# A hybrid RWKV-7 and attention encoder layer: TensorE's order written out for the scan and the attention, both scan directions in one stage, value products one key tile behind their transposes

## The chip, the cores and the metric

The kernel runs on one core of one Trainium2 chip. The metric is device time in microseconds (us). A NeuronCore has five engines that each run their own list of instructions: TensorE (PE in the profile; PEld is its loading of stationary operands), VectorE (DVE), ScalarE (ACT), GpSimd (POOL) and SyncE (SP, which here only issues transfers). They meet through semaphores.

## The reference

One encoder layer over 2304 tokens (a prompt of 256 and a sample of 2048, independent of each other), width 1024. After an RMSNorm and an input projection, half of the columns go through a bidirectional RWKV-7 scan (8 heads of 64), the other half through grouped-query attention (8 query heads, 2 key heads). Then output projection, SwiGLU FFN and norms. The parts that the change touches:

```python
def step(S, inp):                                   # forward and reverse, 8 heads
    r_t, w_t, k_t, v_t, a_t, b_t = inp
    sa = jnp.einsum('bhvk,bhk->bhv', S, a_t)
    S = S * w_t[:, :, None, :] + sa[..., None] * b_t[:, :, None, :] + v_t[..., None] * k_t[:, :, None, :]
    return S, jnp.einsum('bhvk,bhk->bhv', S, r_t)
...
y = y_f + y_b
...
s = jnp.einsum('bqhgd,bkhd->bhgqk', q_blk, k).astype(jnp.float32) * scale
p = jax.nn.softmax(s, axis=-1).astype(v.dtype)
return jnp.einsum('bhgqk,bkhd->bqhgd', p, v)
```

## The kernel before

`build` (L1276) runs in stages: input projection with the preparation of the scan (`e_phase`), the scan with attention beside it, what is left of attention, and the FFN. Stages are Python generators. `beside(g, rate)` (L1328) advances attention by `rate` steps for each step of `g`, so the two are woven together in the source. The source order is not the final one: the tile layer is opened with a scheduler that orders every engine's list by its own model of durations (L1396).

**The scan.** The tokens are 36 chunks of 64 (32 of the sample, then 4 of the prompt). Step k treats one chunk forward and another one backward. For each direction `scan_prep` (L624) loads the chunk's operands, makes the Gram products (L657, eight matmuls into two PSUM tiles `g`), masks them on VectorE (L661, L663) and transposes `bk` (L668). `scan_chain` (L686) is the serial part: for each direction four stages of eight 64-wide matmuls into that direction's half of `hb`: L705, then a ScalarE copy, L711, two copies, L717, the new state on VectorE (L720, L722), and the output L730 with L733. `scan_sv` (L672) sets the state as the next step's operand. `scan_out` (L752) normalizes finished tiles.

**The block inverses.** A chunk needs the inverse of a triangular matrix. `inverses` (L610) makes them for ten (block group, direction) pairs, one after the other: 62 dependent small operations on VectorE or GpSimd (L565, L567), a copy (L570), a round trip through DRAM, and four groups of products (L597, a mask L599, L604). The next pair takes over the previous one's buffers, so that it starts after the last L597. Pairs (0, 0) and (4, 1) are needed at the first chunk, (1, 0) and (3, 1) at the seventh, (3, 0) and (1, 1) at the nineteenth. `scan` pulls the generator `back` three times per round, and empties it as far as needed where a chunk's inverse is missing (L810).

**Attention.** For a key head and a tile of 128 queries, `att_scores` (L853) walks over 16 units (4 key blocks x 4 heads; a prompt tile has 4). A unit is two score products (L880, L881) into `as`, a maximum (L882, VectorE) and an exponential (L884, ScalarE). Then come small softmax operations (L890 to L897), and GpSimd scales the 16 results `p` (L901). `att_values` (L904) takes 128 keys at a time: four transposes into `at` (L913), a split into a high part (ScalarE, L175) and a low part (VectorE, L181), two products into `ao` (L916 with the high, L917 with the low part). `as` and `at` have two PSUM buffers each. `attention` (L927) takes one value step of the previous tile after each score unit.

Of the kernel before, what the change touches and what calls it, by code (L numbers as in the profile page):

```python
# [43 lines left out]
RATE_E, RATE_S = 1.0, 2.75  # L44
# [52 lines left out]
class Kern:  # L97
# [308 lines left out]
    def e_dir(self, e, p, d):  # L406
# [52 lines left out]
        for c in range(nch):  # L459
            for h in range(2):  # L460
# [5 lines left out]
        pool.tensor_scalar(out=self.wc[d][:, p, ch0:ch0 + nch], in0=e1[:, :nch, 64 - 64 * d], scalar1=1.0, scalar2=0.0,  # L466
                           op0=ALU.mult, op1=ALU.add)
# [156 lines left out]
    def scan_prep(self, d, c, sb, ps):  # L624

        nc = self.nc
        act, dve = nc.scalar, nc.vector
        bi, j = self.blk(c)
        gr, off = BLOCKS[bi][2:]
        cs = slice(j * P, j * P + P)  # L630
        q_ = self.sq = getattr(self, "sq", {})
# [3 lines left out]
        ar = self.ard[d][bi]  # L635
        cl = T("cl", [P, 2, 4, P], 4)
        for e in range(2):
            rows = slice(e * 64, e * 64 + 64)
            self.ld(cl[rows, e], ar[:, rows, cs].rearrange("q p t -> p q t"))
        bk = T("bk_", [P, 4, P], 2)  # L640
        self.ld(bk, self.bkd[d][bi][:, :, cs].rearrange("q p t -> p q t"))
        x = T("x_", [P, 4, C], 3)
        for e in range(2):
            self.ld(x[e * 64:e * 64 + 64], self.xd[d][gr][:, e, off + j].rearrange("q s t -> s q t"))
        sav = T("sav", [P, 4, 2, C], 3)
        v = self.vtd[bi][j * C:(j + 1) * C, :]
        self.ld(sav[64:128].rearrange("p q e c -> p (q e c)"), v)
        gm = self.c["gmask_" + "fb"[d]]
        mrb = T("mrb", [C, 4, 2, C], 4)
        bkt = T("bkt", [P, 4, P], 3)  # L650
        q_[d, c] = dict(cl=cl, x=x, sav=sav, mrb=mrb, bkt=bkt, v=v.rearrange("t (q e c) -> t q e c", e=2, c=C))
        yield
# [5 lines left out]
        for e in range(2):  # L658
            other = slice(64 - e * 64, 128 - e * 64)
            psg = psgs[e]  # L660
            dve.tensor_tensor(out=cl[other, e], in0=psg[64:128], op=ALU.mult,  # L661
                              in1=gm[64:128].rearrange("p (o t) -> p o t", o=1).broadcast_to([64, 4, P]))
            dve.tensor_tensor(out=mrb[:, :, e, :], in0=psg[0:64, :, 64:128], op=ALU.mult,  # L663
                              in1=gm[0:64, 64:128].rearrange("p (o t) -> p o t", o=1).broadcast_to([64, 4, C]))
            yield
        psg = ps.tile([P, 4, P], F32, name="g", tag="g", bufs=2)
        for q in range(4):
            nc.tensor.transpose(psg[:, q, :], bk[:, q, :], self.ident)  # L668
        act.copy(out=bkt, in_=psg)
        yield  # L670

    def scan_sv(self, d, c, st, sb):  # L672

        sv = sb.tile([P, 4, 2, C], F32, name="sv", tag=f"sv{d}", bufs=2)
        v = self.sq[d, c]["v"]
        self.ld(sv[64:128, :, 0, :], v[:, :, 0, :])
        self.ld(sv[0:64, :, 1, :], v[:, :, 1, :])
        if st[0] is None:
            st[0] = sb.tile([P, 4, C], F32, name="sc", tag=f"sc{d}", bufs=2)
            self.nc.gpsimd.memset(st[0], 0.0)  # L680
        self.nc.scalar.copy(out=sv[0:64, :, 0, :], in_=st[0][0:64])
        self.nc.gpsimd.tensor_scalar(out=sv[64:128, :, 1, :], in0=st[0][64:128], scalar1=1.0, scalar2=0.0, op0=ALU.mult,
                                     op1=ALU.add)
        st[1] = sv

    def scan_chain(self, d, c, nxt, st, first, sb, ps):  # L686
# [3 lines left out]
        o = self.sq[d, c]  # L690
        cl, x, sav, mrb, bkt = (o[k] for k in ("cl", "x", "sav", "mrb", "bkt"))

        def T(tag, shape, bufs):
            return sb.tile(shape, F32, name=tag, tag=tag, bufs=bufs)
        if st[1] is None:
            self.scan_sv(d, c, st, sb)
        sv = st[1]
        heads = [(h // 2, h % 2, slice(h % 2 * 64, h % 2 * 64 + 64)) for h in range(8)]

        
        def H():
            return self.hb[:, d]
        psa = H()
        for q, e, rows in heads:
            nc.tensor.matmul(psa[rows, q, :], cl[:, e, q, 0:64], sv[:, q, e, :], start=True, stop=True)  # L705
        ry = T("ry", [P, 4, C], 2)
        act.copy(out=ry, in_=psa)
        yield
        psx = H()
        for q, e, rows in heads:  # L710
            nc.tensor.matmul(psx[rows, q, :], x[rows, q, :], ry[rows, q, :], start=True, stop=True)  # L711
        act.copy(out=sav[0:64, :, 0, :], in_=psx[0:64])
        act.copy(out=sav[0:64, :, 1, :], in_=psx[64:128])
        yield
        pss = H()
        for q, e, rows in heads:
            nc.tensor.matmul(pss[rows, q, :], bkt[:, q, rows], sav[:, q, e, :], start=True, stop=True)  # L717

        t = T("st", [P, 4, C], 1)
        dve.tensor_tensor(out=t, in0=pss, in1=st[0], op=ALU.add)  # L720
        sc = sb.tile([P, 4, C], F32, name="sc", tag=f"sc{d}", bufs=2)
        dve.tensor_tensor(out=sc, in0=t, in1=self.wc[d][:, :, c:c + 1].broadcast_to([P, 4, C]), op=ALU.mult)  # L722
        st[0] = sc
        if nxt is not None:
            self.scan_sv(d, nxt, st, sb)
        yield
        psy = H()

        for q, e, rows in heads:
# [670 lines left out]
```

## Time and profile before

| | us |
|---|---|
| median of 3 runs (lowest, highest) | 4079.66 (4074.95, 4089.16) |
| the profiled execution, its own time | 4076.95 |
| span of its instructions | 4074.8 |

The granted TensorE clock had a mean of 0.976 of 2.4 GHz. The scan's first Gram product starts at 1010 us, its last chain product at 2222 us, the last value product of attention ends at 2281 us, and the FFN's matmuls start at 2295 us.

How to read the views: the page sums an execution; a windows view gives the busy time of each engine in a stretch; a timeline lists instructions in order of time, with equal neighbours merged, their start and duration, and in brackets the engine's idle time before them and what ended it; a waits view sums those idle times. Matmul ends are modelled, so PE's starts and PEld's idle times tell more than PE's busy time.

### The profile page before, as it was taken

Reading aid. Unit: us, or ns where it says so; the run is one execution under the profiler, and the core shown is the slowest. Engines: PE = TensorE matmul, PEld = TensorE weight load, DVE = VectorE, ACT = ScalarE, POOL = GpSimd, SP = SyncE. Lnnn points to the kernel's source line nnn. Section 1 sums busy time; section 2 is a strip of 40 time slices with the busy share of each in tenths; the row PEclk is TensorE's granted clock in tenths of the full one; section 3 lists DMA queues with packets and bytes.
Section 4 is the critical chain, followed back from the end, with each engine's and each line's share of the span. In section 5 each row is a group of like instructions: output and inputs, shape, how many; then the busy total and the mean of one; then the engine's idle time right before and its main releaser. Section 6 shows DMA issues by size and latency. Waiting matters only on the chain.

```text
span 4074.8 us, 71176 instructions
## 1 busy us (share of the span) xinstructions
PE 3880.8 (95%) x26208; PEld 3336.7 (82%) x26208; DVE 2866.1 (70%) x4553; ACT 2005.5 (49%) x3940; POOL 1257.7 (31%) x1776
## 2 busy tenths in 40 slices
PE   8999999979999999999999889999989999999998
PEld 7987878746777777777777689998889988799987
DVE  5478586899889776898887577754477744577643
ACT  4345444456666655656666344443344433344432
POOL 2245353543223556734433122200122200212100
PEclk9999999979999999999999999999999999999999
DMA  6567566662433455444441423243423253422251
GB/s 200 166 204 228 173 207 192 207 165 59 101 74 86 92 120 118 114 109 104 109 111 43 146 86 104 96 181 109 166 93 104 96 184 110 159 87 96 102 181 67
DMA packets 646876, 524.32 MB, mean 129 GB/s; under 512 B 368512, under 2 KB 555520, under 8 KB 646528
## 3 DMA queue, kind: packets, MB, share of 16 engines
q1 hardware_dynamic: 577264, 438.36, 36.2%
q0 software_dynamic: 16944, 68.43, 5.1%
q10 hardware_dynamic: 52320, 12.98, 1.5%
q8 instruction: 207, 3.39, 0.3%
q14 instruction: 141, 1.16, 0.1%
HBM read 355.59 MB, written 166.37 MB: 128 GB/s over the span
## 4 chain that ended last, share of the span: by engine, by line
PE 76%; DVE 9%; DMA 4%; POOL 4%; issue 3%; ACT 3%; SPq 1%; ACTq 0%; DVEq 0%; POOLq 0%
PE acc L1082 23%; PE acc L211 8%; PE acc L212 8%; PE acc L213 8%; PE at L913 5%; PE g L657 3%; PE ao L917 3%; PE ao L916 3%; PE as L880 3%; PE as L881 2%; DVE nm L882 1%; DVE ptl L181 1%; PE hb L705 1%; PE hb L730 1%; PE g L597 1%
## 5 line engine op out<-in xcount | busy, mean ns | idle before, releaser
L1082 PE MATMUL acc<-H,wsh 128*128 128x384 f32 x3168 | 814.6, 337 | 32.6 <-ACT cg L1110 23.0
L1082 PEld LDWEIGHTS acc<-H,wsh 128*128 128x128 f32 x3168 | 578.7, 190 | 36.2 <-ACT cg L1110 24.1
L1082 PE MATMUL acc<-H,wsl 128*128 128x384 f32 x1584 | 533.2, 337 | 0.0
L901 POOL TENSOR_SCALAR p<-p,f 128x512 f32<-128x512 f32 (+1 forms) x528 | 372.8, 728 | 284.8 <-DVE f L897 235.9
L884 ACT ACTIVATE p<-as,nm 128x512 f32<-128x512 f32 (+1 forms) x528 | 360.9, 684 | 162.4 <-DVE nm L882 133.8
L211 PE MATMUL acc<-wsh,H 128*128 128x512 f32 x1080 | 419.8, 391 | 14.6 <-ACT wsh L175 14.6
L212 PE MATMUL acc<-wsl,H 128*128 128x512 f32 x1080 | 420.6, 390 | 0.0
L213 PE MATMUL acc<-wsh,H 128*128 128x512 f32 x1080 | 415.6, 389 | 0.0
L175 ACT CAST pth<-at 128x512 fp32r<-128x512 f32 x520 | 300.1, 586 | 228.7 <-PE at L913 223.2
L181 DVE TENSOR_TENSOR ptl<-at,pth 128x512 fp32r<-128x512 f32 x520 | 353.4, 683 | 75.8 <-ACT pth L175 73.4
L882 DVE TENSOR_REDUCE nm<-as 128x1 f32<-128x512 f32 (+1 forms) x528 | 353.0, 674 | 75.2 <-PE as L881 72.7
L211 PE MATMUL acc<-hThi,wih 128*128 128x384 f32 x1008 | 351.5, 349 | 0.8 <-ACT hThi L175 0.7
L212 PE MATMUL acc<-hTlo,wih 128*128 128x384 f32 x1008 | 348.5, 346 | 0.0
L213 PE MATMUL acc<-hThi,wil 128*128 128x384 f32 x1008 | 348.3, 345 | 0.0
L913 PE MATMUL at<-ident,p 128*128 128x128 f32 x2080 | 326.5, 277 | 2.9 <-POOL p L901 2.5
L913 PEld LDWEIGHTS at<-ident,p 128*128 128x128 f32 x2080 | 262.3, 142 | 68.2 <-POOL p L901 6.1
L181 DVE TENSOR_TENSOR wsl<-wsr,wsh 128x1024 fp32r<-128x1024 f32 x156 | 190.9, 1224 | 170.8 <-ACT wsh L175 170.7
L175 ACT CAST wsh<-wsr 128x1024 fp32r<-128x1024 f32 x156 | 164.1, 1052 | 297.9 <-PE acc L1082 151.8
L1082 PEld LDWEIGHTS acc<-H,wsl 128*128 128x128 f32 x1584 | 300.4, 190 | 0.0
L1025 POOL TENSOR_TENSOR sw<-wsr 128x512 f32<-128x512 f32 x66 | 89.2, 1352 | 643.8 <-DVE wsl L181 552.8
L880 PE MATMUL as<-kh,qs 128*128 128x512 f32 (+1 forms) x528 | 248.4, 471 | 31.8 <-ACT p L884 25.6
L181 DVE TENSOR_TENSOR wsl<-sw,wsh 128x1024 fp32r<-128x1024 f32 x132 | 161.2, 1221 | 138.3 <-ACT wsh L175 138.1
(661 smaller groups left out, 8375.1 us busy)
## 6 DMA issues: line engine op xcount, KB each, us to landing
wsr<-in_ffn_gate SPq DMA_DIRECT2D x66, 512.0 KB, 3.5
wsr<-in_ffn_up SPq DMA_DIRECT2D x66, 512.0 KB, 3.8
wsr<-in_ffn_down SPq DMA_DIRECT2D x66, 512.0 KB, 3.6
wir<-in_w_in POOLq DMA_DIRECT2D x63, 512.0 KB, 4.5
hd<-hid POOLq DMA_DIRECT2D x66, 384.0 KB, 3.8
H<-hd SPq DMA_DIRECT2D x33, 768.0 KB, 6.0
cl<-ard SPq DMA_DIRECT2D x144, 128.0 KB, 2.9
zT<-z SPq DMA_DIRECT2D x84, 192.0 KB, 2.7
```

The costliest lines, as they stand in the source:

```text
L175: nc.scalar.copy(out=hi, in_=src)
L181: e.tensor_tensor(out=lo, in0=src, in1=hi.bitcast(F32), op=ALU.subtract)
L211: mm(out, ahi, bhi, start=first, stop=False)
L212: mm(out, ahi, blo, start=False, stop=False)
L213: mm(out, alo, bhi, start=False, stop=last)
L657: nc.tensor.matmul(psgs[e][:, q, :], bk[rows, q, :], cl[rows, e, q, :], start=True, stop=True)
L880: nc.tensor.matmul(pss[:, :hw], qs[:, h, :], kh, start=True, stop=False)
L882: dve.tensor_reduce(out=nm[:, h, i:i + 1], in_=pss[:, :hw], axis=AX.X, op=ALU.max, negate=True)
L884: act.activation(out=p_[:, :hw], in_=pss[:, :hw], func=AF.Exp, bias=nm[:, h, i:i + 1], accum_out=ls[:, h, i:i + 1])
L901: pool.tensor_scalar(out=t, in0=t, scalar1=f[:, h, i:i + 1], scalar2=1.0, op0=ALU.mult, op1=ALU.mult)
L913: nc.tensor.transpose(tp[:, h, :], pt[h, i][:, k * P:(k + 1) * P], self.ident)
L1082: nc.tensor.matmul(acc, x[l][:, k, :], y_[r][:, k, :], start=first and k == 0 and i == 0, stop=k == 3 and i == 2, skip_group_check=True)
```

## The change

TensorE's list is taken out of the scheduler's hands for the scan and for the rest of attention (`manual_schedule`): there its instructions stand in the order of the source. The other engines are still ordered by the scheduler. The source is rewritten to go with it:

- A scan stage covers both directions: 16 matmuls instead of twice 8, one ScalarE or VectorE operation over 512 columns instead of two over 256. The output (L739, L742 of the new source) follows the state product (L728) at once and goes to a `g` tile. Decay factors are stored in step order, so that one operation reads both directions.
- A step is written as: stage 1, Gram products of the next step's forward chunk, attention; stage 2, the backward Gram products, attention; stage 3 and the output, attention; transposes, loads for the step after the next, attention. Each attention part is four turns at a rate of 0.86 units. From step 4 on each turn also pulls `back` once.
- Attention: the transposes of key tile n+1 stand ahead of the products of key tile n; a tile's value products start 3.5 units (`ATT_LAG`) after its last score unit; the query tile is loaded and transposed during the tile before it. At the head change all value products are emptied ahead of the new keys.

The number of matmuls is the same.

```diff
-RATE_E, RATE_S = 1.0, 2.75
+ATT_LAG = 3
+RATE_E, RATE_S = 1.0, 0.86
...
+        heads = [(d, h // 2, h % 2, slice(h % 2 * 64, h % 2 * 64 + 64)) for d in range(2) for h in range(8)]
+        for d, q, e, rows in heads:
+            nc.tensor.matmul(hb[rows, d, q, :], cl[d][:, e, q, 0:64], sv[:, d, q, e, :], start=True, stop=True)
+        ry = T("ry", [P, 2, 4, C], 1)
+        act.copy(out=ry, in_=hb)
+        yield
...
+        def rest(k):
+            for i in range(4):
+                if k > 3:
                     next(back, None)
-            return [self.scan_prep(d, c, sb, ps) for d, c, _, _ in steps[k]]
...
+        for k, step in enumerate(steps):
...
+            for d in range(2):
+                next(chain)
+                if not last:
+                    self.scan_gram(steps[k + 1], d, ps)
+                yield from rest(k)
+            next(chain)
+            yield from rest(k)
+            if not last:
+                self.scan_turn(steps[k + 1], sb, ps)
+            load(k + 2)
+            for i, _ in enumerate(rest(k)):
...
-        for i, k in keys:
+        def turned(i, k):
             tp = ps.tile([P, 4, P], F32, name="at", tag="at", bufs=2)
...
+        hl = [turned(*keys[0])]
+        for n, (i, k) in enumerate(keys):
+            if n + 1 < len(keys):
+                hl.append(turned(*keys[n + 1]))
+            yield
             lhs = kv[parts[i]][2][:, k].rearrange("p a c -> p (a c)")
-            nc.tensor.matmul(pso, lhs, hi, start=(i, k) == keys[0], stop=False)
-            nc.tensor.matmul(pso, lhs, lo, start=False, stop=(i, k) == keys[-1])
-            yield
+            for m, t in enumerate(hl[n]):
+                nc.tensor.matmul(pso, lhs, t, start=n + m == 0, stop=n + m == len(keys))
+            if n + 1 < len(keys):
+                yield
...
+                if not pend:
+                    pend.append(iter(range(2 * ATT_LAG + 1)))
+                pend.append(self.att_values(g, j * P, kv, self.att_p, sb, ps))
...
-                beside(self.scan(back, sb, ps), RATE_S)
+                with tc.manual_schedule(engines={mybir.EngineType.PE}):
+                    beside(self.scan(back, sb, ps), RATE_S)
...
-            run(att)
+            with tc.manual_schedule(engines={mybir.EngineType.PE}):
+                run(att)
```

`load(k)` of the new source pulls `back` without a turn of attention until the inverses of step k's chunks are there, like L810 before.

TensorE's list in a scan step of the kernel before, second stage (L711) of one direction and then of the other; L913 are the value transposes, L880 and L881 score products, L916 and L917 value products:

```order
L711 MATMUL hb<-ry,x__15695 64x64 x8
L657 MATMUL g<-cl,bk__16213 128x128 x4
L668 MATMUL g<-ident,bk__16201 128x128 x4
L917 MATMUL ao<-ptl,vst_8787 128x512
L916 MATMUL ao<-pth,vst_8787 128x512
L913 MATMUL at<-ident,p 128x128 x4
L880 MATMUL as<-kh_8812,qs 128x512
L881 MATMUL as<-kl_8813,qs 128x512
L711 MATMUL hb<-ry,x__15707 64x64 x8
```

The same place after the change (L722 is the second stage, L663 the Gram products, L950 the transposes, L917 and L918 the score products, L960 both value products):

```order
L722 MATMUL hb<-ry,x__15044 64x64 x8
L722 MATMUL hb<-ry,x__15053 64x64 x8
L663 MATMUL g<-cl,bk__15531 128x128 x8
L950 MATMUL at<-ident,p 128x128 x4
L917 MATMUL as<-kh_8814,qs 128x512
L918 MATMUL as<-kl_8815,qs 128x512
L960 MATMUL ao<-pth,vst_8789 128x512
L960 MATMUL ao<-ptl,vst_8789 128x512
L950 MATMUL at<-ident,p 128x128 x4
```

Both directions now stand together, and attention comes in the fixed pattern transposes, scores, values. The second place is where the inverses of pair (3, 1) are finished. Before, TensorE has attention between the product groups L597 and L604:

```order
L597 MATMUL g<-i_12821,i_12820 128x128 x4
L917 MATMUL ao<-ptl,vst_8760 128x512
L913 MATMUL at<-ident,p 128x128 x4
L880 MATMUL as<-kh_8812,qs 128x512
L881 MATMUL as<-kl_8813,qs 128x512
L916 MATMUL ao<-pth,vst_8760 128x512
L917 MATMUL ao<-ptl,vst_8760 128x512
L913 MATMUL at<-ident,p 128x128 x4
L880 MATMUL as<-kh_8812,qs 128x512
L881 MATMUL as<-kl_8813,qs 128x512
L604 MATMUL g<-xqt,am 128x32 x4
```

After, at the end of the fifth step (k = 4), the last two groups of pair (1, 0) (buffers 12902 to 12907) and the first two of pair (3, 1) (13044 to 13049); the eight groups of both pairs stand in one row, with attention only behind them:

```order
L601 MATMUL g<-i_12907,i_12906 128x128 x4
L608 MATMUL g<-xqt,am 128x32 x4
L601 MATMUL g<-i_12907,i_12906 128x128 x4
L608 MATMUL g<-xqt,am 128x32 x4
L601 MATMUL g<-i_13045,i_13044 128x128 x4
L608 MATMUL g<-xqt,am 128x32 x4
L601 MATMUL g<-i_13045,i_13044 128x128 x4
L608 MATMUL g<-xqt,am 128x32 x4
```

VectorE's list at that place after the change (L603 is the mask between the two products, L569 and L571 the serial operations of pair (3, 1)):

```order
L182 TENSOR_TENSOR ptl<-at,pth 128x512
L603 TENSOR_TENSOR am<-g,cst 128x512 x4
L569 TENSOR_TENSOR i_12971<-i_12967,i_12970 128x31
L571 TENSOR_TENSOR i_12970<-i_12970,i_12971 128x31
L569 TENSOR_TENSOR i_12971<-i_12967,i_12970 128x30x2
L571 TENSOR_TENSOR i_12970<-i_12970,i_12971 128x30x2
```

All 62 operations of the pair follow each other without a row of attention or scan, and the copy L574 and four L603 come behind them; before, 75 other rows stood among the 62. At the end of step 16 the four groups of pair (1, 1) stand in one row likewise; the other pairs have attention between their groups.

## Rows read from the trace of the kernel before

**Rows 1.** The page: span, and engine, busy us, share, instructions.

```profile
span 4074.8 us, 71176 instructions
PE 3880.8 (95%) x26208; PEld 3336.7 (82%) x26208; DVE 2866.1 (70%) x4553; ACT 2005.5 (49%) x3940; POOL 1257.7 (31%) x1776
```

**Rows 2.** Windows view: PE, PEld, DVE, ACT, POOL busy (count), clock, DMA share, GB/s.

```profile
1010.00:1165.00 155.00, 150.55 (x1505) 121.36 (x1505) 131.66 (x280) 93.82 (x238) 44.35 (x68) 1.00 0.40 98
1165.00:1250.00 85.00, 78.03 (x553) 59.08 (x552) 75.89 (x165) 55.93 (x136) 26.16 (x36) 0.94 0.33 69
1250.00:1640.00 390.00, 379.20 (x3757) 306.36 (x3756) 294.80 (x564) 232.11 (x572) 209.62 (x358) 0.98 0.46 106
1640.00:2222.00 582.00, 561.98 (x5551) 439.16 (x5552) 497.83 (x967) 372.76 (x908) 249.01 (x369) 1.00 0.39 99
2222.00:2288.00 66.00, 51.80 (x257) 36.24 (x255) 43.62 (x80) 35.58 (x77) 27.92 (x39) 0.93 0.12 29
2288.00:2306.00 18.00, 10.39 (x36) 8.07 (x36) 4.92 (x5) 4.97 (x6) 0.00 (x0) 0.70 0.97 372
```

**Rows 3.** Timeline of PEld in one scan step, 1508 to 1530 us.

```profile
1509.44 0.55 PEld L730 LDWEIGHTS hb<-sv,cl 128*64 128x64 f32 x16 [0.25 <-DVE sc L722]
1510.06 0.54 PEld L733 LDWEIGHTS hb<-sav,mrb 64*64 64x64 f32 x16
1510.67 0.19 PEld L917 LDWEIGHTS ao<-ptl,vst 128*128 128x128 f32 x1
1510.78 0.19 PEld L880 LDWEIGHTS as<-kh,qs 128*128 128x128 f32 x1
...
1528.13 0.56 PEld L913 LDWEIGHTS at<-ident,p 128*128 128x128 f32 x4
...
1528.78 0.19 PEld L880 LDWEIGHTS as<-kh,qs 128*128 128x128 f32 x1
1529.02 0.19 PEld L881 LDWEIGHTS as<-kl,qs 128*128 128x128 f32 x1
...
1529.48 0.59 PEld L913 LDWEIGHTS at<-ident,p 128*128 128x128 f32 x4
```

**Rows 4.** Waits view of PEld, 1010 to 2288 us: total, times, longest.

```profile
PEld as L880 <- ACT p L884: 32.8, 46, 1.9
PEld ao L917 <- DVE ptl L181: 22.5, 39, 2.5
PEld g L657 <- issue: 14.1, 42, 1.6
PEld hb L705 <- issue: 14.0, 55, 0.4
PEld hb L711 <- issue: 9.9, 44, 0.4
PEld hb L730 <- issue: 8.1, 35, 0.4
PEld hb L717 <- issue: 7.8, 33, 0.4
PEld ao L916 <- ACT pth L175: 5.1, 16, 0.8
PEld at L913 <- POOL p L901: 3.8, 10, 1.0
PEld as L880 <- DVE qs L872: 3.6, 6, 1.6
PEld g L657 <- PE as L881: 3.4, 7, 1.2
PEld g L657 <- PE at L913: 2.8, 8, 0.5
PEld g L657 <- DMA cl<-ard: 2.7, 3, 1.3
```

**Rows 5.** Windows view of lines L565 and L567 alone, pair (3, 1).

```profile
1160.00:1235.00 75.00, 11.39 (x31) 0.00 (x0) 0.93 0.28 66
1160.00:1235.00 75.00, 11.57 (x31) 0.00 (x0) 0.93 0.28 66
```

**Rows 6.** Timeline of DVE and PEld: pair (3, 1), first operations, copy, products.

```profile
1165.10 0.20 DVE L565 TENSOR_TENSOR i<-i,i 128x31 f32<-128x31 f32 x1
1165.34 0.23 DVE L567 TENSOR_TENSOR i<-i,i 128x31 f32<-128x31 f32 x1
...
1228.64 1.23 DVE L570 COPY i<-i 128x1024 f32<-128x1024 f32 x1
1238.39 0.68 DVE L599 TENSOR_TENSOR am<-g,cst 128x512 f32<-128x512 f32 x1
...
1237.08 0.96 PEld L597 LDWEIGHTS g<-i,i 32*128 32x128 f32 x8 [0.37 <-issue]
1255.14 0.97 PEld L604 LDWEIGHTS g<-xqt,am 128*128 128x128 f32 x8
```

**Rows 7.** Timelines: softmax operations and scaling for two tiles, and key loads.

```profile
1340.55 0.16 DVE L890 TENSOR_REDUCE mx<-nm 128x4 f32<-128x16 f32 x1
1342.34 4.72 POOL L901 TENSOR_SCALAR p<-p,f 128x512 f32<-128x512 f32 x7 [2.64 <-DVE f L897]
...
1784.17 0.15 DVE L890 TENSOR_REDUCE mx<-nm 128x4 f32<-128x16 f32 x1
1796.12 4.02 POOL L901 TENSOR_SCALAR p<-p,f 128x512 f32<-128x512 f32 x4
...
1533.72 0.19 PEld L880 LDWEIGHTS as<-kh,qs 128*128 128x128 f32 x1
1536.04 0.20 PEld L847 LDWEIGHTS as<-ident,kdup 128*128 128x128 f32 x2
1541.25 0.71 PEld L847 LDWEIGHTS as<-ident,kdup 128*128 128x128 f32 x4
1572.79 0.19 PEld L880 LDWEIGHTS as<-kh,qs 128*128 128x128 f32 x1
```

**Rows 8.** The page's transfers, and the timeline of SP late in the scan.

```profile
cl<-ard SPq DMA_DIRECT2D x144, 128.0 KB, 2.9
...
1884.51 2.48 SPq L110 DMA_DIRECT2D yT<-ov  x4
1887.09 0.54 SPq L104 DMA_DIRECT2D bk__22776<-bkd  x1
```

More of the change, by code (lines that the diff above doesn't have):

```diff
@@ L669, in scan_prep, with scan_turn @@
[L669 to L677, printed above, removed]
+    def scan_turn(self, step, sb, ps):
+        o = self.sq[step["c"]]
+        for bk in o["bk"]:
+            psg = ps.tile([P, 4, P], F32, name="g", tag="g", bufs=2)
+            for q in range(4):
+                self.nc.tensor.transpose(psg[:, q, :], bk[:, q, :], self.ident)
+            bkt = sb.tile([P, 4, P], F32, name="bkt", tag="bkt", bufs=3)
+            self.nc.scalar.copy(out=bkt, in_=psg)
+            o["bkt"].append(bkt)
@@ L695, in scan_chain @@
         if st[1] is None:
-            self.scan_sv(d, c, st, sb)
+            self.scan_sv(step, st, sb)
         sv = st[1]
[L698 to L707, printed above, removed]
-        yield
@@ L709, in scan_chain @@
[L709 to L713, printed above, removed]
-        yield
[L715 to L720, printed above, removed]
@@ L812, in scan @@
[L812 to L827 removed]
+            st = [None, None]
@@ new lines, in scan, with load @@
+            steps += [dict(c=(lo + i, hi - 1 - i), at=lo + i, st=st, first=2 * i < n) for i in range(n)]
+        def load(k):
+            if k < len(steps):
+                for d, c in enumerate(steps[k]["c"]):
+                    while (BLOCKS[self.blk(c)[0]][2], d) not in self.ready:
+                        next(back, None)
+                self.scan_load(steps[k], sb)
+        def rest(k):
+            for i in range(4):
+                if k > 3:
+                    next(back, None)
+                yield
@@ new lines, in scan @@
+        load(0)
+        for d in range(2):
+            self.scan_gram(steps[0], d, ps)
+            yield
+        self.scan_turn(steps[0], sb, ps)
+        load(1)
+        yield
+        for k, step in enumerate(steps):
+            last = k + 1 == len(steps)
+            self.outs = []
+            chain = self.scan_chain(step, None if last or steps[k + 1]["st"] is not step["st"] else steps[k + 1], sb, ps)
+            for d in range(2):
+                next(chain)
[8 more added lines that the diff above has]
+            for i, _ in enumerate(rest(k)):
+                if i == 2:
+                    for g in self.outs:
+                        next(g, None)
+                yield
@@ L1307, in build @@
             self.consts(cp)
-            self.wc = [cp.tile([P, 4, NCH], F32, name=f"wc{d}") for d in range(2)]
+            self.wc = cp.tile([P, 2, 4, NCH], F32, name="wc")
             ec, esb, eps = pools(st_e, "e", "right")
@@ L1338, in build, with early @@
             beside(eg, RATE_E)
+            def early():
+                while any(b not in self.ready for b in ((0, 0), (4, 1))):
+                    next(back)
+                    yield
+            beside(early(), 0.5)
             st_e.close()
```

229 lines of the change are left out of this document (125 added, 104 removed).

## The prediction

> **What bounds the kernel now.** I read the page first. TensorE is busy 95% of the span, VectorE 70%, ScalarE 49% [rows 1]. That asks where TensorE's 5% and its modelled busy time hide waits, so the windows view came next: the change reaches 1010 to 2288 us, 1278 us of the span, and there VectorE is busy between 66% (66 us at the end) and 89% (the 85 us of one inverse pair); in the longest stage it is 497.83 of 582 us and ScalarE 372.76 [rows 2]. TensorE bounds this part, but VectorE is not far behind it, so a better order can gain only until VectorE is full.
>
> Then I looked at how TensorE issues. In the timeline of the weight loads an undisturbed unit of attention (four transposes, two scores, two value products) takes 1.35 us, from the first transposes at 1528.13 to the next at 1529.48. A group of eight chain matmuls shows as 16 loads of 0.55 us in all; the next group starts 0.62 us after it, and there is a pause ahead of the first [rows 3]. Last I read the waits of the weight loads. Three things stand there: scores that wait for an exponential (a free `as` buffer) or for the query split, 32.8 and 3.6; value products and transposes that wait for the split or for `p`, 22.5, 5.1 and 3.8; and pauses ahead of chain groups and Gram products that nothing releases [rows 4].
>
> **The change, part by part.** The number of matmuls stays, so each term is a pause that goes or comes. Minus is a gain. The steps are 36.
>
> *Joint stages: -47 us.* Before, a step has ten groups of 0.62 = 6.2 us. After, it has five of twice the size. By the weight loads alone one takes 2 x 0.55 = 1.10, by two old groups 1.24 [rows 3]; I take 1.12, since within a group the loads follow each other without a gap: 5.6, so 0.6 less. The pauses: the four rows "hb <- issue" are 39.8 us in 167 cases, 0.24 each [rows 4]. Before there are 8 entries a step (output follows output), after it 3: five go, 1.2 us. Part is no gain: behind a group the score's load came 0.11 us after its neighbour, in the undisturbed unit 0.24 [rows 3], so 0.13 of each pause is made up now. That leaves 0.11 to 0.24 each, 0.55 to 1.2 a step; I take 0.7. Together 1.3 x 36 = 47, bounds 20 (lesser pause alone) and 68.
>
> *Attention's order: -45 us.* The five waits of attention sum to 67.8 us [rows 4]. In the new order two value products, two scores and the next transposes stand between a key tile's transposes and its products, almost a whole unit of 1.35 us, and a scan piece interrupts after every 3.44 units (4 turns x 0.86) and lets the other engines catch up. VectorE and ScalarE have room for it (86% and 64% in the longest stage [rows 2]). I take two thirds of it, as the buffers stay at two; bounds 0 and 68.
>
> *Gram products: -12 us.* Their waits are 14.1 + 3.4 + 2.8 + 2.7 = 23.0 us [rows 4]. They now stand in fixed places where both `g` tiles have been free for a quarter of a step. Half of it; bounds 0 and 23.
>
> *Pairs (1, 0) and (3, 1) at the end of step 4: +41 us.* This is the main cost. Eight product groups stand in TensorE's list with nothing between them. Pair (3, 1) can only start when the last group of (1, 0) has read its buffers, and its own groups stand right behind, so TensorE stands still for the whole series. Nothing covers it, since attention stands behind. VectorE has it for itself: 11.39 + 11.57 = 23.0 us for the 62 operations [rows 5], about 2 for their gaps (1165.10, 0.20 long, to 1165.34 leaves 0.04), the copy 1.2, the round trip from the copy's end at 1229.9 to the first product at 1237.1, 7.2 [rows 6]. A group takes 0.96 + 0.68 + 0.97 and two hand-overs, 2.9, of which 1.93 are TensorE's own work, done before too; eight groups idle for 8 x 0.97 = 7.8. Sum 41. The lower bound is 34 (the round trip hidden by half, groups overlapped); the upper one is what the pair took under load, 1165.1 to 1256.1, 91 us [rows 6]. That pair (1, 0) is ready by then rests on four steps of lead.
>
> By the Trainium skill ("TensorE: Matmul & The Clock Gate", section "Part 3: Packing small matmuls — row/col tiling", under its measured speedups) matmuls start and end strictly in program order, and only weight loads are pulled ahead. If attention could pass the waiting product, this term would be 0 and the time 41 us lower; by the page it can't. No row of before tests this, since the scheduler put no such wait there.
>
> *Pair (1, 1) at the end of step 16: +4 us.* Four groups in a row, 4 x 0.97 idle [rows 6]; its series runs on GpSimd from step 14 on and should be done. Upper bound 25: round trip exposed and a third of the series left.
>
> *The head change: +6 us.* Before, 39 us pass from the last score of the first head (1533.72) to the first of the second (1572.79), with key blocks 5.2 us apart and values and scan between them [rows 7]. After, the values are emptied first and three key blocks stand in a row: up to 3 x (5.2 - 0.7) = 14 us idle, of which the kernel before lost part too. Bounds 0 and 14.
>
> *Values that start 3.5 units behind: +5 us.* Those units are 4.7 us, with the scan piece between them about 7. The first four of the scaled `p` came 4.5 us after the first softmax operation in one tile (1342.34 + 4 x 0.67 - 1340.55) and 16.0 us in another (1800.14 - 1784.17) [rows 7]: the first is hidden, the second waits 9 us. Before, `p` cost 3.8 us in all [rows 4], the scheduler having had other work. Bounds 0 and 34 (one tile in eight of about 30 like the second).
>
> *Costed at nothing.* ScalarE's and VectorE's wider operations: these engines are not the bound [rows 2]; if VectorE were, its stages would shrink a little. Loads for the step after the next: the last one ahead of the Gram product, `bk`, waits for the transposes just ahead, then has 3.44 units and stage 1, 4.6 + 1.1 = 5.7 us, against an issue of 0.6 and a landing of 2.9 [rows 8]. If that cover is gone, TensorE waits in each step. Attention's rate: the scan now takes nearly all of it along, so the 66 us behind the scan [rows 2] shrink while the scan's steps hold more. The FFN's start (13 us of idle TensorE) and the FFN stay.
>
> *The clock.* Before, the window 1165 to 1250 had 0.94 of the clock, 1250 to 1640 0.98, 2222 to 2288 0.93 [rows 2]: 5 + 8 + 5 = 18 us of half speed or less at places where TensorE had paused. After, there are fewer pauses and one long one; I take 0, from -10 to +5 (18 us at 0.70, as at the FFN's start, cost 5.4).
>
> Sum: -47 - 45 - 12 + 41 + 4 + 6 + 5 = -48 us. Against the profiled execution's 4076.95 us that is 4029; the median of the runs is 2.7 above it, so **4032 us**.
>
> **Rivals.** A measurement of this kernel can tell about 0.3%, 12 us, from no change.
>
> 1. *The order gives nearly all it could* (0.16). Attention's and Gram's waits go whole, -68 - 23, with -47 and +56 for the places: -82, 3998 us. For it: both engines have room. Against: VectorE at 86% leaves little slack within a unit.
> 2. *The waits stay, under other names* (0.14). In order, each late split or exponential now holds the scan too. Then only joint stages and the costs count: -47 + 56 = +9, 4089 us. For it: two buffers of `as` and `at` as before. Against: the new distances.
> 3. *The pair's series goes at the old pace* (0.10). 91 instead of 41 us: +2, 4082 us. Against: VectorE's list has no other row among the 62.
> 4. *Slower: the loads come late* (0.10). Place: `bk` ahead of the Gram products. The margin is 5.7 - 3.5 = 2.2 us. SyncE issues at about 0.6 us each [rows 8] in a list that is held by any wait in front; seven issues ahead of `bk` make TensorE wait 2 us a step, 72 in all: +24, 4104 us. It decides from 1.7 us a step on (61 us). Before, the loads cost Gram little (2.7 [rows 4]), but they were further ahead.
>
> The forecast has 0.50, its own range is 4002 to 4064.
>
> **How the numbers follow.** Range: from 3980 (a third of rival 1 outside) to 4096 (rival 4 and a part of rival 2 outside), about 2 in 10 left out; it takes in the bounds of the pair and of attention's waits one at a time. Faster (below 4067): 0.49 of the forecast, 0.16, 0.02 of rival 3: 0.67. Same: 0.01 of the forecast, 0.08 of rival 2, 0.06 of rival 3, 0.01 of rival 4: 0.16. Slower (over 4092): 0.06 + 0.02 + 0.09 = 0.17.
>
> **What would show it.** Joint stages: 32 loads of a chain group in 1.1 us, three entries a step. Attention: waits of its five kinds together under 30 us. Step 4: one TensorE gap around 35 us ahead of pair (3, 1)'s first product, VectorE full of its operations. Step 16: a gap below 10 us. The stretch from the first Gram product to the last value product falls from 1271 to some 1225 us. I would be wrong if waits for VectorE or ScalarE grow in the second half, where `scan_out` adds VectorE work, if Gram products wait for `bk`, or if the pair's gap is far from 41.

## The result, and the profile after

| | us |
|---|---|
| new kernel, median of 4 runs (lowest, highest) | 4287.47 (4285.42, 4290.76) |
| kernel before beside it, median of 4 runs | 4084.41 (4074.95, 4092.47) |
| ratio, 95% interval | 1.050 (1.047 to 1.053): slower |
| the profiled execution of the new kernel, span | 4284.6 |

The forecast was 4032 with a range to 4096. The page answers to [rows 1]: TensorE does the same work, but is busy for 90% instead of 95% of a longer span.

```profile
span 4284.6 us, 70733 instructions
PE 3852.7 (90%) x26208; PEld 3316.2 (77%) x26208; DVE 2881.2 (67%) x4481; ACT 1997.7 (47%) x3778; POOL 1252.2 (29%) x1738
```

The windows view (columns as in [rows 2]) shows where it is less busy. The last value product ends near 2492 instead of 2281 us, and behind it the FFN starts as soon as before, so the 210 us are lost ahead of it:

```profile
1010.00:1165.00 155.00, 132.17 (x1315) 105.16 (x1315) 122.24 (x253) 87.94 (x202) 30.23 (x48) 0.92 0.35 83
1165.00:1265.00 100.00, 58.58 (x437) 49.88 (x437) 56.28 (x130) 24.98 (x62) 13.52 (x21) 0.68 0.34 70
1265.00:1640.00 375.00, 331.07 (x3296) 263.50 (x3295) 276.92 (x503) 224.08 (x505) 182.44 (x301) 0.95 0.36 83
1640.00:2222.00 582.00, 457.20 (x4435) 361.67 (x4436) 413.20 (x761) 296.26 (x672) 227.58 (x342) 0.90 0.37 91
2222.00:2495.00 273.00, 225.20 (x2219) 174.71 (x2218) 198.43 (x352) 158.41 (x350) 91.59 (x127) 0.96 0.24 65
```

In the stretch 1640 to 2222 us TensorE has fallen from 561.98 to 457.20 us of work, VectorE from 497.83 to 413.20, ScalarE from 372.76 to 296.26 [rows 2]. No engine is fuller; all of them wait for each other.

Some 22 us of the loss lie ahead of the scan, at a place for which the prediction has no term. The new source finishes the inverses of the first two pairs, (0, 0) and (4, 1), in a short loop of its own, with half a step of attention per pull; the scan's attention belongs to the fixed list behind it and can't fill in. So TensorE stands still there, and the loads that follow take 1.78 us instead of 0.96 (weight loads):

```profile
1007.38 1.78 PEld L601 LDWEIGHTS pc<-i,i 32*128 32x128 f32 x8 [9.10 <-DMA i<-xpt]
1010.24 1.78 PEld L608 LDWEIGHTS pc<-xqt,am 128*128 128x128 f32 x8 [1.08 <-DVE am L603]
```

The first Gram product comes at 1022.3 us instead of 1009.9, behind 66 score units instead of 73: 12.4 us, and 7 units of 1.35 that are still to be done (an estimate from these counts). With TensorE's list left to the scheduler (the first experiment) the same source has 82 units ahead of the first Gram product, at 1025.4 us.

The waits of the weight loads from 1010 to 2495 us (total, times, longest) answer to [rows 4]:

```profile
PEld ao L960 <- DVE ptl L182: 156.5, 205, 4.1
PEld g L663 <- issue: 51.4, 11, 7.4
PEld as L917 <- ACT p L921: 35.8, 35, 4.3
PEld g L601 <- issue: 32.4, 9, 29.8
PEld ao L960 <- ACT pth L176: 27.4, 39, 3.9
PEld as L892 <- ACT p L921: 18.9, 22, 1.8
PEld g L608 <- issue: 18.4, 15, 2.2
PEld hb L728 <- issue: 11.7, 35, 0.7
PEld hb L722 <- issue: 11.6, 36, 0.7
PEld hb L717 <- issue: 10.3, 32, 0.7
PEld at L950 <- POOL p L938: 3.2, 6, 0.5
```

The chain groups do what was forecast. The pauses ahead of `hb` that nothing releases are 103 with 33.6 us instead of 167 with 39.8, and all waits ahead of `hb` together are 106 with 34.6 us instead of 281 with 75.6. But the low value product now waits 156.5 us for VectorE's split (22.5 before), and the Gram products 51.4 us in only 11 waits. By tile, from 1000 us to the FFN, the waits of the weight loads have risen by 157 us ahead of `ao`, 102 ahead of `g`, 36 ahead of `as` and 13 ahead of `pc`.

**One wait for the split, read from both engines.** Timeline of the new kernel's weight loads (start, duration), stage 1 of one step:

```profile
2148.06 1.01 PEld L717 LDWEIGHTS hb<-sv,cl 128*64 128x64 f32 x32 [0.36 <-DMA qdup<-qd]
2149.14 0.97 PEld L663 LDWEIGHTS g<-cl,bk__23502 64*128 64x128 f32 x16
2150.23 0.42 PEld L950 LDWEIGHTS at<-ident,p 128*128 128x128 f32 x4
...
2152.33 0.19 PEld L960 LDWEIGHTS ao<-pth,vst 128*128 128x128 f32 x1
2153.84 0.19 PEld L960 LDWEIGHTS ao<-ptl,vst 128*128 128x128 f32 x1 [1.33 <-DVE ptl L182]
```

VectorE's timeline at the same time:

```profile
2150.34 0.69 DVE L667 TENSOR_TENSOR cl<-g,cst 64x512 f32<-64x512 f32 x1 [1.65 <-PE g L663]
2151.04 0.42 DVE L669 TENSOR_TENSOR mrb<-g,cst 64x256 f32<-64x256 f32 x1
2151.47 0.69 DVE L667 TENSOR_TENSOR cl<-g,cst 64x512 f32<-64x512 f32 x1
2152.18 0.42 DVE L669 TENSOR_TENSOR mrb<-g,cst 64x256 f32<-64x256 f32 x1
2152.52 0.67 DVE L919 TENSOR_REDUCE nm<-as 128x1 f32<-128x512 f32 x1
2153.12 0.67 DVE L182 TENSOR_TENSOR ptl<-at,pth 128x512 fp32r<-128x512 f32 x1
2153.72 0.68 DVE L919 TENSOR_REDUCE nm<-as 128x1 f32<-128x512 f32 x1
```

While TensorE does the joint stage and the Gram products, VectorE waits (1.65 us for the latter). Then its four masks take 2.2 us, and the next unit's maximum and split stand behind them. A unit needs 1.2 us of VectorE (two operations, 0.6 apart) out of 1.35, so VectorE makes up 0.15 us per unit within attention. By these rows it would need some 15 units to make up for one group of masks (an estimate), and there are two groups in a step of 14 units. TensorE, which takes its list in order, pays.

### The profile page after: what moved, and what is told of

Read it like the earlier page. It is cut to its first block, busy times and chain, and to the rows that moved or that the text cites. A ratio compares the mean times of both kernels' runs of the same rounds, so it can differ in the third digit from the quotient of the medians.

```text
span 4284.6 us, 70733 instructions
## 1 busy us (share of the span) xinstructions
PE 3852.7 (90%) x26208; PEld 3316.2 (77%) x26208; DVE 2881.2 (67%) x4481; ACT 1997.7 (47%) x3778; POOL 1252.2 (29%) x1738
## 3 DMA queue, kind: packets, MB, share of 16 engines
q14 instruction: 139, 1.14, 0.1%
## 4 chain that ended last, share of the span: by engine, by line
PE 64%; DVE 16%; DMA 5%; issue 5%; POOL 4%; ACT 3%; SPq 2%; ACTq 0%; DVEq 0%; POOLq 0%
PE acc L1146 22%; PE acc L212 7%; PE acc L213 7%; PE acc L214 7%; PE ao L960 4%; PE at L950 3%; DVE ptl L182 3%; DVE nm L919 2%; PE g L663 2%; PE as L917 2%; PE as L918 2%; DVE cl L667 2%; DVE i L571 1%; DVE i L569 1%; PE g L601 1%
## 5 line engine op out<-in xcount | busy, mean ns | idle before, releaser
L938 POOL TENSOR_SCALAR p<-p,f 128x512 f32<-128x512 f32 (+1 forms) x528 | 360.6, 705 | 406.4 <-DVE f L934 282.6
L950 PE MATMUL at<-ident,p 128*128 128x128 f32 x2080 | 328.5, 284 | 2.5 <-POOL p L938 2.3
L960 PE MATMUL ao<-ptl,vst 128*128 128x512 f32 x520 | 232.8, 448 | 91.7 <-DVE ptl L182 90.3
L950 PEld LDWEIGHTS at<-ident,p 128*128 128x128 f32 x2080 | 259.0, 146 | 56.8 <-POOL p L938 6.1
L917 PE MATMUL as<-kh,qs 128*128 128x512 f32 (+1 forms) x528 | 259.4, 491 | 34.6 <-ACT p L921 32.4
```

Of the source, the lines that this page charges most:

```text
L917: nc.tensor.matmul(pss[:, :hw], qs[:, h, :], kh, start=True, stop=False)
L938: pool.tensor_scalar(out=t, in0=t, scalar1=f[:, h, i:i + 1], scalar2=1.0, op0=ALU.mult, op1=ALU.mult)
L950: nc.tensor.transpose(tp[:, h, :], pt[h, i][:, k * P:(k + 1) * P], self.ident)
L960: nc.tensor.matmul(pso, lhs, t, start=n + m == 0, stop=n + m == len(keys))
```

## The experiments

Line numbers in rows are those of each kernel's own source. A "turn" is a change from attention's matmuls to the scan's, counted in the weight loads of a trace from the first Gram product to the last chain product: 408 in the kernel before, 174 in the new one. The "fixed order" is the list of the new kernel, in which TensorE's instructions stand in the order of the source.

### Order and source apart

Both `manual_schedule` lines go, all else stays:

```diff
-                with tc.manual_schedule(engines={mybir.EngineType.PE}):
-                    beside(self.scan(back, sb, ps), RATE_S)
+                beside(self.scan(back, sb, ps), RATE_S)
```

> The rewritten source (joint stages, new attention, drained head change) stays; only TensorE's list goes back to the scheduler. Theory A (the fixed order is what costs, the new source by itself gains): 4020 to 4070 us, and the waits of the low value product for VectorE fall from 156 us to under 50. Rival B (the source costs: wide operations, loads for the step after the next, values emptied at the head change): over 4180 us. Between 4090 and 4180 both share.

Measured: 4170.7 us, 1.021 (1.019 to 1.022) of the kernel before; the waits for the split fall to 29.0 us between 1000 and 2500. So the fixed order costs 117 us, and the new source under the scheduler another 86. Neither theory holds alone.

### VectorE's split left out, in both kernels

```diff
-            return self.split(sb, tp.rearrange("p h q -> p (h q)"), [P, 512], "pt", bufs=3)
+            hi = sb.tile([P, 512], F32R, name="pth", tag="pth", bufs=3)
+            act.copy(out=hi, in_=tp.rearrange("p h q -> p (h q)"))
+            return hi, hi
```

> The new kernel without VectorE's split of the transposed probabilities: the second value product multiplies the high part again, so TensorE has the same work and VectorE 0.68 us less for each of 520 key tiles. Theory A1 (TensorE's fixed list waits for VectorE, which is full within a unit): the 156 us of waits go and little replaces them, 4100 to 4150 us. Rival (the waits only change their name, to the cast on ScalarE or to buffers): over 4200 us.

> The control for the run without VectorE's split: the same edit in the kernel before. There the waits for the split were 22.5 + 2.4 us. Theory A1 (only the fixed list makes TensorE wait for VectorE): 4050 to 4075 us, a gain of 10 to 35 us beside 97 in the new kernel. Rival (VectorE's load costs both kernels alike, by the clock or by its other operations): a gain of 70 us or more.

Measured: 4190.5 us in the new kernel, 97 less; 4110.4 in the edited kernel before, which is 1.006 (1.004 to 1.008) of the unedited one, no gain at all. In the new kernel the 156.5 us are gone, and 40 of them come back as waits of the scores for the exponential (35.8 before the edit; waits view, 1000 to 2500 us):

```profile
PEld as L917 <- ACT p L921: 76.0, 77, 4.5
PEld g L663 <- issue: 56.0, 10, 9.0
```

Not all of the 97 us is attention's: with the same 66 units ahead of it, the first Gram product comes at 997.6 instead of 1022.3 us, so 25 of them lie at the place ahead of the scan, where TensorE waits for a series of VectorE's operations.

VectorE's load costs time where TensorE's order is fixed; in the kernel before no gain shows when it goes. That control is not a clean one, since its scheduler made other choices too: its granted clock was 0.960 to 0.965 in the four runs, against 0.970 to 0.975 in those beside it, which may hide a part of the 22.5 us of waits for the split [rows 4] that could be won there. Two rivals are left untested: no run changes the order of VectorE's own list, and none gives `at`, `as` or the split tiles more buffers.

### The head change

```diff
-            while pend:
+            for kv in self.att_kv(g, sb, ps):
                 half()
                 half()
                 yield
-            for kv in self.att_kv(g, sb, ps):
-                yield
```

> The values of the first head are no longer emptied ahead of the second head's keys: two half turns of values follow each key block, the rest runs along with the first scores. Steps 14 to 17 took 41.5, 36.8, 53.8 and 47.1 us, with units missing in them. Theory A2 (emptying costs 60 to 80 us there, since one of scores and values alone can't fill TensorE): 4205 to 4230 us. Rival (the units lost there are only moved, and the waits come back elsewhere): over 4260 us.

Measured: 4283.7 us, 4 less. The place itself is mended: windows of the second score product, steps 14 to 17, of the new kernel and of this one (length, busy, count, clock):

```profile
1603.50:1782.70 179.20, 7.69 (x30) 0.77 0.36 83
```

```profile
1609.20:1799.40 190.20, 10.77 (x50) 0.84 0.36 84
```

Twenty more scores for 11 us. But attention then ran out before the scan. The last score is at 2431.67 and the last value product's load at 2466.39, 25 us sooner than in the new kernel (2491.39). Yet the FFN's first product came at the same time as there (2505.14), after a longer wait for its weights (weight loads):

```profile
2504.64 2.21 PEld L212 LDWEIGHTS acc<-wsh,H 128*128 128x128 f32 x6 [22.21 <-ACT wsh L176]
```

### The row of inverse groups in step 4

In the new kernel the row begins so (weight loads), and ends at 1262 us:

```profile
1196.88 0.96 PEld L601 LDWEIGHTS g<-i,i 32*128 32x128 f32 x8 [0.91 <-ACT bkt L680]
1198.89 0.97 PEld L608 LDWEIGHTS g<-xqt,am 128*128 128x128 f32 x8 [1.04 <-issue]
...
1211.63 1.78 PEld L608 LDWEIGHTS g<-xqt,am 128*128 128x128 f32 x8 [1.14 <-issue]
1243.20 1.77 PEld L601 LDWEIGHTS g<-i,i 32*128 32x128 f32 x8 [29.79 <-issue]
```

The edit pulls the inverses from step 0 on, twice per turn until step 4:

```diff
-                if k > 3:
+                for _ in range(2 if k < 5 else 1):
                     next(back, None)
```

> The inverses are pulled twice per turn in steps 0 to 4, so that the product groups of pairs (1, 0) and (3, 1) stand among attention in steps 1 to 4 and no row of eight groups is left in step 4. Theory A3 (in the row TensorE stood still, 1197 to 1262 us, with 15 us of its own work in it): 50 us less, 4225 to 4245 us, and step 4 about 35 us long. Rival (TensorE then waits for the series at the earlier places, since VectorE must make them beside attention): 4270 us or more.

Measured: 4273.6 us, 14 less. The row of step 4 is gone, but steps 1 to 4 take 200 us, as in the new kernel (198). Window over them:

```profile
1077.50:1277.40 199.90, 161.86 (x1429) 131.35 (x1428) 148.44 (x325) 92.75 (x217) 49.27 (x79) 0.85 0.43 91
```

The granted clock (0.85) is no better than in the same steps of the new kernel (0.84), and a pause of 11.7 us ahead of L601 shows that the products now wait for a series which VectorE makes beside attention: its copy ends at 1160.3 us, and the first product starts at 1167.8. The rival held.

### Two outputs in one step

Here is the longest kind of Gram wait, in the weight loads of the new kernel:

```profile
2108.35 0.29 PEld L663 LDWEIGHTS g<-cl,bk__23006 64*128 64x128 f32 x2
2114.93 1.78 PEld L663 LDWEIGHTS g<-cl,bk__23006 64*128 64x128 f32 x14 [6.28 <-issue]
```

The first product goes, the second needs the other `g` tile. VectorE's timeline tells who holds it:

```profile
2109.10 0.18 DVE L934 TENSOR_TENSOR f<-f,mx 128x16 f32<-128x16 f32 x1
2111.74 0.42 DVE L802 TENSOR_TENSOR yo<-g,yg 128x256 f32<-128x256 f32 x1 [2.47 <-POOL p L938]
2114.43 0.42 DVE L802 TENSOR_TENSOR yo<-g,yg 128x256 f32<-128x256 f32 x1 [2.26 <-DMA yg<-gdr]
```

Two tiles are finished in one step. The second one's transposes hold `g` until VectorE's product, which waits for single buffers (`yo`, `yg`), for GpSimd and for a load; meanwhile VectorE's list stands as well. The edit takes one tile in the last part of a step and the other in the second part of the next:

```diff
-                    for g in self.outs:
-                        next(g, None)
...
+                if out and i == 2 and self.outs:
+                    next(self.outs.pop(0), None)
```

> The new kernel; of two finished tiles only one is transposed in the last part of a step, the other one in the second part of the next step. Theory D (the second tile's transposes hold a g buffer until VectorE's product, which waits for single buffers, GpSimd and the gate's load; the Gram products of the next step stand behind it, 51 us in 11 waits, and VectorE's list stands too): the long Gram waits go, 4220 to 4240 us. Rival (the loads for the step after the next are late, or the work is only moved): over 4270 us, and the Gram waits stay.

Measured: 4228.5 us, 59 less. Gram waits, 1010 to 2440 us, from 51.4 us to

```profile
PEld g L663 <- issue: 4.9, 3, 2.6
```

### Gram products ahead of the joint stage, and everything mended

The first run adds to the one above that `scan_gram` is called ahead of `next(chain)`; the second adds the head change, a rate of 0.84 and another schedule for the inverses.

```diff
+PULLS = {3: (2, 2, 2, 2), 4: (1, 1, 2, 2), 16: (2, 2, 2, 2)}
...
+                for _ in range(PULLS.get(k, (1, 1, 1, 1))[self.part % 4]):
+                    next(back, None)
```

> One finished tile at a time as before (4228 us), and the Gram products stand ahead of the joint stage instead of behind it, so that VectorE's four masks (2.2 us) run beside 1 us of chain products. Theory F (masks and split meet in VectorE's list, and TensorE pays for the masks within the units right behind): up to 1 us for each of 71 Gram groups, 4165 to 4200 us, and the waits of the low value product fall by 25 us or more. Rival (VectorE's total load within the units counts, not where the masks stand): 4215 us or more.

> The fixed order with every place mended: one output at a time, Gram first, values not emptied at the head change with a rate of 0.84, and the inverses pulled once per turn from step 0 on and twice in steps 3, 16 and half of 4, so that the row of eight groups in step 4 shrinks to three pairs of groups and the one in step 16 goes. If the losses are places (65 us in step 4, some 70 in steps 14 to 17) and each can be mended alone: 4060 to 4110 us. Rival (in a fixed order each stall mended uncovers the next, as in the runs with the head change and the earlier inverses): over 4150 us.

Measured: 4191.8 us, 37 less than without it, and the waits for the split fall from 164.5 to 124.8, while the Gram waits rise from 4.9 to 24.3; then 4150.1, 42 less again. Mending works place by place, but the mended fixed order is still 1.015 (1.012 to 1.017) of the kernel before. Without VectorE's split in it:

> The mended fixed order (4150 us) without VectorE's split, the second value product multiplying the high part again. Its waits for the split were 125 us. Theory A1 (what the mended fixed order still loses to the scheduled one, 60 to 90 us, is VectorE's list): 4050 to 4085 us. Rival (the waits change their name, to the exponential and to p): over 4110 us.

Measured: 4059.4 us, 91 less, which is 0.992 (0.990 to 0.994) of the kernel before. Of the 91, 22 lie ahead of the scan (first Gram product at 1000.5 instead of 1022.2 us). What the mended fixed order still lost hangs on VectorE's load.

### What the source costs under the scheduler

> TensorE's list left to the scheduler, and the values not emptied at the head change. With the scheduler alone the time was 4171 us, 86 above the kernel before, and steps 15 to 18 held almost no transposes or no scores (48, 19, 38, 37 us at clocks down to 0.65). Theory C (what the source costs by itself is the emptied head change): 4080 to 4115 us. Rival (another part of the source costs, joint stages or the new attention): over 4140 us.

Measured: 4184.1 us. The head change was not it. With the new scan source and the attention of the kernel before, all left to the scheduler:

> The scan of the new source (joint stages, output into a g tile, loads for the step after the next) with the attention of the kernel before, and all lists left to the scheduler. Theory E (joint stages gain as forecast, if nothing else is changed): 4035 to 4065 us. Rival (the scheduler takes the joint groups apart, or the new scan gains nothing): 4080 us or more.

Measured: 4175.7 us, so the scan source has the whole cost. The timeline of its weight loads shows what the scheduler makes of a joint group (L728, L739 and L742 are stage 3 and the output):

```profile
2111.51 0.20 PEld L728 LDWEIGHTS hb<-sav,bkt 128*64 128x64 f32 x4 [0.17 <-issue]
2111.62 0.20 PEld L739 LDWEIGHTS g<-sv,cl 128*64 128x64 f32 x2
2111.88 0.19 PEld L910 LDWEIGHTS as<-kh,qs 128*128 128x128 f32 x1
2111.99 0.19 PEld L911 LDWEIGHTS as<-kl,qs 128*128 128x128 f32 x1
2112.55 0.55 PEld L739 LDWEIGHTS g<-sv,cl 128*64 128x64 f32 x16 [0.36 <-issue]
2113.16 0.19 PEld L910 LDWEIGHTS as<-kh,qs 128*128 128x128 f32 x1
...
2113.82 0.31 PEld L739 LDWEIGHTS g<-sv,cl 128*64 128x64 f32 x8 [0.36 <-issue]
```

A group of 32 loads is cut into pieces of 2 to 16, and a return to the scan has its pause: 568 turns in all. The next edit leaves the order to the scheduler, but pins a group's matmuls together (used for stages, Gram products and transposes; stage 1 and the Gram products also take the odd heads first, whose operand or tile comes last). The first matmul of a group has no pin, and in the traces about half of the Gram groups are cut behind it:

```diff
+    def glued(self, mm):
+        with self.tc.manual_schedule(engines={mybir.EngineType.PE}):
+            mm[0]()
+            with self.tc.high_priority(GLUE):
+                for m in mm[1:]:
+                    m()
```

> The new scan source with the attention of the kernel before, all left to the scheduler: 4176 us with the joint groups taken apart (565 turns). Now with whole groups (289 turns), nothing else changed. Theory J (the turns cost): 70 to 120 us less, 4055 to 4105 us. Rival (the one output at a time made the gain in the run with whole groups, not the turns): over 4140 us.

> TensorE's list left to the scheduler (4171 to 4184 us in three runs), but the matmuls of a joint stage, of a Gram group and of a transposition are pinned together, so that TensorE turns from attention to the scan about 290 times instead of 560 (about 410 in the kernel before, 190 in the fixed order); one output at a time. Theory J (each turn costs 0.25 us by its pause and up to 0.55 by the two kernels' second halves, 137 turns more and 75 us more): 4025 to 4110 us. Rival (something else in the new scan source costs, such as the loads or the wide operations, and the turns are cheap): over 4150 us.

> The kernel before with nothing changed but that the matmuls of a stage of one direction, of a Gram group and of a transposition are pinned together: about 320 turns from attention to the scan instead of 410. Theory J (each turn taken away gives 0.25 to 0.55 us): 22 to 50 us less, 4035 to 4065 us. Rival (the scheduler's other choices move with it and eat it up): 4075 us or more.

| kernel | turns in the trace | us | less, per turn less | pauses ahead of the turns |
|---|---|---|---|---|
| new scan source, groups cut, then whole | 568, 296 | 4175.7, 4100.5 | 75.2 / 272 = 0.28 us | 139.8, 94.3 us |
| kernel before, then with whole groups | 408, 378 | 4089.3, 4061.4 | 27.9 / 30 = 0.93 us | 100.9, 105.4 us |

The new source whole, with the new attention and one output at a time, has 4091.0 us, 1.001 (0.999 to 1.002) of the kernel before. The kernel before with whole groups is 0.993 (0.992 to 0.995) of it: faster than both kernels, with its two directions apart. The expectation reckoned with about 320 turns there; the trace has 378. So the two pairs don't agree on a price of a turn. In the first pair 46 of the 75 us are pauses ahead of turns that went. In the second these pauses didn't fall at all, so its 28 us came otherwise, by a part of the edit or by the scheduler's other choices; the cause stays open.

> The scheduled kernel with whole groups and one output at a time (4091 us), with a rate of 1.0 instead of 0.86. There the scan's last step began at 2160 us, 36 us before that of the kernel before, and attention was left behind it. Theory K (the scan ran ahead, and attention alone behind it is worth less): 4060 to 4080 us, with the scan's end and attention's end closer together. Rival (the sum of the work counts): 4085 us or more.

> As the run with a rate of 1.0, and the values not emptied at the head change. In the scheduled kernel with shredded groups this changed nothing (4171 to 4184 us). Theory (emptying costs only where TensorE has too little else): within 10 us of the run with a rate of 1.0. Rival (with whole groups it shows): 15 us or more less.

> The kernel before with whole groups (4061 us) at a rate of 3.0 instead of 2.75, so that more attention lies beside the scan. About 340 turns instead of 320. Theory J: 5 us more by the turns, and up to 15 us less by a shorter rest of attention behind the scan: 4050 to 4070 us. Rival (the rest behind the scan costs nothing): 4061 us or more.

Measured: 4078.1 us, 13 less than at a rate of 0.86; 4073.5 with the head change, within the spread of it; and 4063.5 for the kernel before at a rate of 3.0, no difference from 4061.4.

## Why the prediction was wrong, point by point

- **Attention's order, -45 us: the step that failed.** The five waits are not under 30 us but 156.5 + 35.8 + 27.4 + 3.2 and 2.0 for the query split, 225 us against 67.8, with 18.9 more for the query transposes. The step said that VectorE and ScalarE "have room for it", by shares of 86% and 64% in the longest stage, and that a scan piece "lets the other engines catch up". The 86% is an average over units and scan pieces. Within a unit VectorE has 0.15 us of 1.35 to spare, and behind a scan piece comes its burst of masks, not a rest. The runs without the split in the fixed order (97 and 91 us, of which 25 and 22 lie ahead of the first Gram product) and the one with the Gram products moved (37) show it. Rival 2 named this mechanism, but priced it as the old waits at their old size.
- **Gram products, -12 us: failed too.** It rested on `g` tiles that "have been free for a quarter of a step". From the second half of the scan on the last quarter holds the transposes of two finished tiles; 51.4 us instead of 11, and 59 us given back when they were taken apart. Rival 4 had a late load in mind there; the load that was late was the gate's, `yg`, not `bk`.
- **The place ahead of the scan: no term.** Some 22 us, by the later first Gram product and the 7 units that were still to be done.
- **Joint stages, -47 us: right.** A group of 32 loads takes 1.01 us (1.10 forecast), and there are 3 entries a step. All waits ahead of `hb` fell by 41 us, where the forecast had 1.2 x 36 = 43 before what is made up behind a group. What of it reached the time can't be told apart here. Among the scheduled kernels with whole groups the one with the directions apart is the fastest; why the new scan source costs some 39 us there (4100.5 against 4061.4) stays open but for the rate, which gave 13 in the kernel with whole groups and one output at a time.
- **Pairs (1, 0) and (3, 1), +41 us: right.** The row took 1197 to 1262 us, 65, with 15.4 of TensorE's own work in it (eight groups of 1.93 at the clock of before): 50. The gap ahead of pair (3, 1) is 29.79, the round trip from the copy's end (1235.9) to the product 7.3 (7.2 forecast), a hand-over 1.04 to 1.14 (0.97). What was missing is the clock: the loads grow from 0.96 to 1.78 us within the row, and the window from 1165 to 1265 us has 0.68 of full speed. By the Trainium skill ("TensorE: Matmul & The Clock Gate", "Part 3: Packing small matmuls — row/col tiling") matmuls keep program order; this trace agrees, since no matmul of attention went ahead in those 65 us. The one schedule that only pulled earlier gave back 14 of the 50.
- **Pair (1, 1), +4 us: right.** Four pauses of 0.99 to 1.14 us.
- **The head change, +6 us.** The place lost far more (30 score units in four steps instead of 50), yet mending it returned 4: attention ended 25 us sooner, and the FFN's start did not move. Its price hangs on what bounds the end.
- **Values 3.5 units behind, +5 us: smaller.** The waits for `p` are 3.2 us in all (3.8 before).
- **The clock, 0: failed.** The mean is 0.951 instead of 0.976, and from the first Gram product to the last value product 0.91 instead of 0.99. The lowest windows are those of the places above (0.68 in the row of step 4, 0.77 at the head change). What the clock costs by itself no run tells apart from the pauses.

As a sum: in the fixed order the runs took back 59 us (outputs), 37 (masks), 42 (head change, inverses, rate) and 91 (split), 228 in all against the 203 that the change cost. The last of them leaves out a part of the work that the kernel needs; without that, 137 us came back.

## What to carry to other kernels

Before a scheduler's order is replaced by a fixed one, add up each other engine's time within one unit of the fixed pattern, and what its bursts put ahead of the operation that the pattern waits for; an average share over a stage says nothing on that. A fixed list turns every late operand anywhere into a wait of everything behind it, so places have to be mended one by one, and each shows the next. If the gain looked for is whole groups, pinning the groups and leaving the rest to the scheduler is the smaller step: here that, with odd heads first, took 28 us off the kernel before, though the traces don't show that it came from fewer turns.

## What the runs showed of the hardware that was not expected

The pause ahead of a scan piece goes with the shape of its first matmul, not with the change of work. In the trace of the kernel before, from the first Gram product to the last chain product, 332 turns go from attention's 128x128 loads to the scan's smaller shapes (128x64, 64x64, 64x128, 32x128); 327 of them have a pause of more than 0.15 us, with a median of 0.25. The other 76 go to 128x128 loads of the scan, its transposes and the second products of the inverses; 1 of them has such a pause. By the Trainium skill ("TensorEngine Tiling (Array Packing)", "Key Properties") a change of tiling mode drains TensorE; the pauses agree with it. What a turn costs the kernel as a whole is not shown: 0.28 us in one pair of kernels, 0.93 in the other.

The granted clock falls within rows of small groups, ahead of the large gap. In step 4 it is 0.98 of full speed, 2.4 GHz, from 1196.8 to 1200.9 us and 0.50, 1.2 GHz, from 1202.2 on, behind two pauses of 1.0 to 1.1 us; the loads go from 0.97 to 1.78 us. In step 16 it is 1.00 from 1715.3 to 1719.3 and 0.50 from 1720.4 on, likewise behind two such pauses.
